# Branch projections by seven products, in one stream of weight steps with output projection and MLP

## The chip, the core and the metric

The kernel runs on one core of a Trainium2 chip. TensorE (PE in the profile) multiplies, with its weight loads on PEld; VectorE (DVE), ScalarE (ACT) and GpSimd (POOL) do the elementwise work; SyncE (SP) issues nearly all DMAs, ScalarE a few. The metric is device time of one execution in microseconds (us).

## What is computed

The reference is one decoder layer for 1024 tokens of width 1024, cut here to its frame. The three branches are a chunked mLSTM (M), a differential attention (D) and an attention to 256 memory tokens (C).

```python
h = rms_norm(x, norm_mix_g)
y_m, y_d, y_c = mlstm(h @ w_in[...]), diff_attention(h @ w_in[...]), cross_attention(h @ w_in[...], mem)
g_m, g_d, g_c = split(sigmoid(h @ w_gate + b_gate), 3)
merged = g_m * (y_m @ w_proj_m) + g_d * (y_d @ w_proj_d) + g_c * (y_c @ w_proj_c)
x = x + merged @ w_out
h2 = rms_norm(x, norm_mlp_g)
return x + square(relu(h2 @ w_up)) @ w_down
```

All weights of projections are 1024 x 1024; w_up is 1024 x 4096 and w_down 4096 x 1024. Everything is float32.

## The kernel before

Each float32 operand is split into two parts of lower precision: ACT casts the high part and DVE subtracts it for the low part (`split`, `split2`, lines 102 to 115). A product is then three matmuls (`mm3`, line 117): high times high, high times low, low times high. Activations lie transposed, features on the partitions and 512 tokens (one half, `hf`) in a matmul's columns.

The stages run one after the other on TensorE: norm and branch C, then branch M, 64 steps of gate groups, branch D, the rest of the gate groups, the three branch projections, the output projection, the MLP's up half and its down half. The gates come from a generator, `gate_steps`: each `next` gives one step of three matmuls `mm<-hT,w`. Steps are put between the branches' own work; a finished group passes ACT's tanh of half its value (`gt`, a sigmoid up to a factor) and is stored to DRAM (`gates<-gt`). Branch D projects a head group, turns queries and keys by PE (`pr`) into one buffer (`dsg`), sends that through SP's DMAs into `dq` and `dk`, and multiplies these to scores (`sc<-dk,dq`).

`tail` (line 1297) does the projections. It loads the branch's output (`kraw<-y`), splits it (`kt`) and goes through four column groups of 256 with eight k of 128 and four PSUM banks each (`group`, line 1274): 3 x 4 x 4 x 8 x 3 = 1152 matmuls `mm<-kt,w`. DVE multiplies a bank by 1 + gate (`gl`), POOL adds into `mg`; the sum is split into `mh` and `ml` and multiplied by `w_out` in 384 matmuls. Its use adds x, stores `x1_d` and, scaled, `h2_d`, and POOL sums the squares for the norm.

Up and down (`wino`, line 1174; `down`, line 1445) use a seven-product scheme. A pair of 128-blocks of k, a pair of column blocks and two halves of the tokens form 2 x 2 blocks; seven products of sums of blocks take the place of eight. The weights' sums are made by POOL (`wino_s`, four operations on 128x128, into `wraw`), the operands' by DVE and POOL (`wino_t`, `xts`); then all are split. A run is one output block: 4 pairs of k, 7 products of 3 matmuls each, 84 matmuls, into seven of PSUM's eight banks, so that a run's product can start when the run before has been read out of the bank. `PROD` is the order of products. The step table (`wino_steps`) loads and splits weights some steps ahead.

Where `pinned` is set, or an engine is wrapped in `InOrder`, instructions stand on their engine in the order in which the code writes them; elsewhere a scheduler sets the order. In both cases each engine and each DMA queue takes its instructions in that order. Tile pools hand out buffers; a pool that is opened in memory of a closed one makes its first writers wait for the last users of that memory.

After up, each output block passes the norm's scale (`rb`), relu and square (`rq`), and is stored with its sums (`r_d<-rq`, `r_d<-xts`); down loads it back (`xd<-r_d`), adds its four passes of each group in `acc` tiles, whose start is `x1_d` (`acc<-x_d`), and writes out.

Of the kernel before, what the change touches and what calls it, by code (L numbers as in the profile page):

```python
# [71 lines left out]
class Layer:  # L72
    def __init__(self, tc, a, out):
        self.tc, self.nc, self.a, self.out = tc, tc.nc, a, out
        self.V, self.A = InOrder(tc, tc.nc.vector), tc.nc.scalar
        self.n = 0
# [1044 lines left out]
    PROD = ((0, 0), (1, 2), (4, 4), (5, 5), (2, 6), (3, 3), (6, 1))  # L1121

    def wino_t(self, b, V):

        G = self.nc.gpsimd
        t = self.xtp.tile([P, 4, 512], F32, tag="xt", name=self.name("xts"))
        V.tensor_sub(t[:, 0], b[:, 0], b[:, 1])
        G.tensor_sub(t[:, 2], b[:, 2], b[:, 0])
        V.tensor_sub(t[:, 1], b[:, 2], t[:, 0])
        V.tensor_sub(t[:, 3], b[:, 3], t[:, 1])  # L1130
        return t

    def wino_x(self, kp, load):

        b = load(kp)
        t = self.wino_t(b, self.nc.vector)
        xo = self.xop[kp].tile([P, 7, 2, 512], F32R, tag="xo", name=self.name("xo"))
        self.split(xo[:, 0:3, 0], xo[:, 0:3, 1], b[:, 1:4])
        self.split(xo[:, 3:7, 0], xo[:, 3:7, 1], t)
        return xo  # L1140

    def wino_s(self, r):

        G = self.nc.gpsimd
        G.tensor_add(r[:, 4], r[:, 0], r[:, 3])  # L1145
        G.tensor_sub(r[:, 5], r[:, 4], r[:, 1])  # L1146
        G.tensor_sub(r[:, 6], r[:, 1], r[:, 0])  # L1147
        G.tensor_sub(r[:, 7], r[:, 2], r[:, 5])  # L1148

    def wino_steps(self, srcs, wrp, wop, lead):  # L1150


        raws, W = [], []

        def raw():
            n = len(raws)
            if n < len(srcs):
                r = wrp.tile([P, 8, P], F32, tag="wraw", name=self.name("wraw"))
                self.nc.sync.dma_start(r[:, 0:4], srcs[n])
                self.wino_s(r)  # L1160
                raws.append(r)

        def wsp(n, split=self.split2, more=True):
            m = len(W)
            if m < len(srcs) and m <= n + lead:
                wo = wop.tile([P, 7, 2, P], F32R, tag="wo", name=self.name("wo"))
                split(wo[:, :, 0], wo[:, :, 1], raws[m][:, 1:8])
                W.append(wo)
# [602 lines left out]
```

## Time and profile before

| what | us |
|---|---|
| runs: median of 3 | 2213.95 (2213.91 to 2215.54) |
| the profiled execution | 2213.57 |
| its span | 2211.8 |
| TensorE busy | 2163.4 (98%) |
| VectorE, ScalarE, GpSimd busy | 62%, 44%, 24% |
| 64 gate steps ahead of branch D, 192 matmuls | 575.5 to 620 |
| branch projections | 1218.5 to 1482.4 |
| output projection | 1482.4 to 1575.2 |
| up | 1575.2 to 1891.8 |
| down | 1891.8 to 2207.5 |

In rows of the profile, a group has its line of the code, its engine and operation, what it writes and reads, the count, then busy us and mean ns of one, and the idle time of the engine ahead of it with what ended it. A timeline row has its start, its length, and the same names. "SPq" rows are SP issuing DMAs.

### The profile page before, as it was taken

The page shows a single profiled execution, that of the slowest core. Times are in us where ns is not written, and L with a number is a line of the kernel's source. Part 1 is how long each engine was busy: PE and PEld are TensorE (multiplying, and loading weights), DVE is VectorE, ACT ScalarE, POOL GpSimd, SP SyncE. Part 2 cuts the span into 40 slices and gives each one's busy share as a digit, 9 for nine tenths or more (in the row PEclk, how much of TensorE's full clock was granted, in tenths as well). Part 3 has the DMA queues.
Part 4 walks back from the last instruction along what each step waited for, and adds up shares of the span by engine and source line. Part 5 has one row for each costly group of instructions (what it writes and reads, how often), then busy time and mean ns, then how long its engine had stood idle before and what let it go on. Part 6 is the DMA issues. An engine that isn't in the chain of part 4 may idle for free.

```text
span 2211.8 us, 30588 instructions
## 1 busy us (share of the span) xinstructions
PE 2163.4 (98%) x11097; PEld 1860.7 (84%) x11097; DVE 1361.4 (62%) x2598; ACT 980.7 (44%) x1962; POOL 527.8 (24%) x696
## 2 busy tenths in 40 slices
PE   7999999999999999999999999999999999899999
PEld 5878888898899999999888888877787888688887
DVE  6643575565237777777641232544688877767779
ACT  6543355454336666666542120223444444543332
POOL 2100000000011111111000003202557655565553
PEclk9999999999999999999999999999999999999999
DMA  7023122121333333333343443436435444854444
GB/s 250 29 81 115 50 91 76 44 82 39 107 109 86 93 84 84 88 92 86 101 148 114 134 142 126 138 110 205 147 115 198 159 147 147 318 196 146 145 145 170
DMA packets 127948, 273.06 MB, mean 123 GB/s; under 512 B 12945, under 2 KB 21430, under 8 KB 125750
## 3 DMA queue, kind: packets, MB, share of 16 engines
q1 hardware_dynamic: 125494, 258.53, 37.2%
q10 hardware_dynamic: 2304, 12.58, 1.4%
q8 instruction: 87, 1.43, 0.3%
q14 instruction: 63, 0.52, 0.1%
HBM read 178.76 MB, written 67.14 MB: 111 GB/s over the span
## 4 chain that ended last, share of the span: by engine, by line
PE 77%; DVE 9%; DMA 6%; ACT 4%; issue 2%; POOL 2%; SPq 0%; DVEq 0%; ACTq 0%; POOLq 0%
PE mm L91 46%; PE p L91 20%; PE sc L91 6%; PE tp L94 2%; PE po L91 2%; DVE acc L67 1%; DMA kraw<-y 1%; DMA xr<-h_d 1%; DVE wo L67 1%; DMA y<-yd 1%; DVE u L67 1%; DVE w L112 1%; DMA wraw<-in_wup 0%; DVE xts L67 0%; DVE c L67 0%
## 5 line engine op out<-in xcount | busy, mean ns | idle before, releaser
L91 PE MATMUL mm<-w,hT 128*128 128x384 f32 (+3 forms) x2496 | 473.4, 332 | 8.3 <-DVE dsg L112 5.4
L91 PE MATMUL mm<-hT,w 128*128 128x512 f32 x1920 | 465.7, 395 | 0.0
L91 PEld LDWEIGHTS mm<-hT,w 128*128 128x128 f32 x1920 | 353.5, 188 | 74.2
L91 PEld LDWEIGHTS mm<-w,hT 128*128 128x128 f32 x2496 | 389.2, 190 | 22.2 <-DVE dsg L112 7.6
L91 PE MATMUL p<-xd,wo 128*128 128x512 f32 x1344 | 310.0, 393 | 5.7 <-DVE c L67 2.2
L91 PE MATMUL p<-xo,wo 128*128 128x512 f32 x1344 | 308.2, 390 | 5.7 <-DVE st L1418 2.6
L91 PEld LDWEIGHTS p<-xd,wo 128*128 128x128 f32 x1344 | 253.8, 189 | 61.7 <-DVE c L67 3.3
L91 PEld LDWEIGHTS p<-xo,wo 128*128 128x128 f32 x1344 | 251.0, 188 | 61.5 <-DVE u L67 3.7
L91 PE MATMUL mm<-kt,w 128*128 128x512 f32 x1152 | 262.2, 389 | 1.9 <-ACT w L111 1.1
L112 DVE TENSOR_TENSOR w<-raw,w 128x256 fp32r<-128x256 f32 (+3 forms) x304 | 173.0, 590 | 137.9 <-ACT w L111 136.8
L91 PEld LDWEIGHTS mm<-kt,w 128*128 128x128 f32 x1152 | 216.0, 188 | 47.9 <-ACT w L111 1.5
L111 ACT CAST w<-raw 128x256 fp32r<-128x256 f32 (+3 forms) x304 | 154.3, 530 | 178.9 <-PE mm L91 114.5
L104 ACT CAST wo<-wraw 128x896 fp32r<-128x896 f32 x122 | 115.0, 945 | 208.9 <-PE p L91 115.2
L67 DVE TENSOR_TENSOR wo<-wraw,wo 128x896 fp32r<-128x896 f32 x122 | 143.7, 1195 | 59.4 <-ACT wo L104 59.4
L1145 POOL TENSOR_TENSOR wraw<-wraw 128x128 f32<-128x128 f32 x128 | 97.3, 760 | 245.8 <-DMA wraw<-in_wdown 108.1
L1007 ACT ACTIVATE dpe<-sc,dst,drr 128x256 f32<-128x256 f32 (+7 forms) x128 | 106.7, 834 | 99.7 <-DVE dst L1003 92.0
L999 DVE CUSTOM_DVE_ANT_0 sc<-sc,tmask 128x256 f32<-128x256 f32 (+7 forms) x128 | 97.0, 758 | 12.6 <-PE sc L91 12.5
L127 POOL TENSOR_SCALAR hss<-hss 128x4 f32<-128x4 f32 x8 | 3.3, 410 | 415.4 <-ACT mscr L752 272.9
L91 PE MATMUL sc<-dk,dq 128*128 128x512 f32 (+3 forms) x384 | 90.4, 343 | 0.0
L1148 POOL TENSOR_TENSOR wraw<-wraw 128x128 f32<-128x128 f32 x128 | 85.6, 669 | 10.0
L1146 POOL TENSOR_TENSOR wraw<-wraw 128x128 f32<-128x128 f32 x128 | 87.3, 682 | 0.0
L1147 POOL TENSOR_TENSOR wraw<-wraw 128x128 f32<-128x128 f32 x128 | 87.2, 682 | 0.0
(283 smaller groups left out, 2832.6 us busy)
## 6 DMA issues: line engine op xcount, KB each, us to landing
dk<-dsg SPq DMA_DIRECT2D x64, 256.0 KB, 4.4
wraw<-in_wup SPq DMA_DIRECT2D x64, 256.0 KB, 3.4
r_d<-xts SPq DMA_DIRECT2D x16, 1024.0 KB, 4.1
wraw<-in_wdown SPq DMA_DIRECT2D x64, 256.0 KB, 3.1
xd<-r_d SPq DMA_DIRECT2D x19, 768.0 KB, 7.4
xd<-r_d SPq DMA_DIRECT2D x14, 1024.0 KB, 6.8
raw<-in_wgate SPq DMA_DIRECT2D x48, 256.0 KB, 3.2
gates<-gt SPq DMA_DIRECT2D x48, 256.0 KB, 2.0
```

What stands on the lines that cost most here:

```text
L67: return self.tc.keep_in_program_order(f(*a, **k))
L91: self.pin(self.nc.tensor.matmul(out, l, r, start=start, stop=stop))
L94: self.pin(self.nc.tensor.transpose(out, x, self.ident))
L104: self.A.copy(hi, src)
L111: nc.scalar.copy(hi, src)
L112: nc.vector.tensor_sub(lo, src, f32(hi))
L999: V.tensor_tensor_reduce(out=sc[:, 0:n], in0=sc[:, 0:n], in1=self.tmask[:, D - n : D], scale=1.0, scalar=-3.0e38, op0=ALU.add, op1=ALU.max ...
L1007: nc.scalar.activation(pe[c][:, 0:n], sc[:, 0:n], AF.Exp, bias=t8[:, 2 + c : 3 + c], scale=rr[:, i, c : c + 1], accum_out=t8[:, 4 + c : 5 ...
L1145: G.tensor_add(r[:, 4], r[:, 0], r[:, 3])
L1146: G.tensor_sub(r[:, 5], r[:, 4], r[:, 1])
L1147: G.tensor_sub(r[:, 6], r[:, 1], r[:, 0])
L1148: G.tensor_sub(r[:, 7], r[:, 2], r[:, 5])
```

## The change

`tail`, `wino`, `wino_steps` and `down` are replaced by one function, `stream`. All weights from the branch projections on are one list of steps (48 of branches, 12 of the output projection, 64 each of up and down), loaded two steps at a time into two buffers and split three steps ahead into three. Every branch projection is four runs of 84 matmuls, in the order C, M, D. Operand tiles lie in slots that stages share (`SLOT`). The accumulators of down are placed in the left pool after `o`, the pool of `rq` and `xts`, has been closed.

The operands' sums of the branches are made ahead by `x_jobs` and kept in DRAM (`xtC_d`, `xtM_d`, `xtD_d`): C's and M's in eight jobs under the 64 gate steps, D's in eight half-jobs under the gate steps behind branch D. The counts in `waits` are gate steps between load, sums, store and the next load. `wino_t` works in place in a job. The first two operands and weights of the stream are prepared under the gates too (`s_early`).

```diff
+        self.G, self.S = InOrder(tc, tc.nc.gpsimd), InOrder(tc, tc.nc.sync)
...
-    PROD = ((0, 0), (1, 2), (4, 4), (5, 5), (2, 6), (3, 3), (6, 1))
+    PROD = ((1, 0), (2, 2), (5, 5), (0, 3), (3, 6), (4, 4), (6, 1))
+    SLOT = {"C": "ABCD", "M": "EABC", "D": "DEAB", "U": "ABHF", "N": "GABF"}
+    def wino_t(self, b, t, V, G):
+        V.tensor_sub(t[:, 1], b[:, 0], b[:, 1])
+        G.tensor_sub(t[:, 0], b[:, 2], b[:, 0])
+        V.tensor_sub(t[:, 2], b[:, 2], t[:, 1])
+        V.tensor_sub(t[:, 3], b[:, 3], t[:, 2])
+
+    def x_jobs(self, pool, jobs, n, waits):
+        nc = self.nc
+        for s, kp in jobs:
+            for c in range(0, 512, n):
+                r = pool.tile([P, 4, n], F32, tag="xj", name=self.name("xj"))
+                for k in range(2):
+                    src = self.yd[self.YOF[s]][2 * kp + k].rearrange("p (h n) -> p h n", h=2)
+                    self.S.dma_start(r[:, 2 * k : 2 * k + 2], src[:, :, c : c + n])
+                for _ in range(waits[0]):
+                    yield
+                self.wino_t(r, r, nc.vector, nc.gpsimd)
+                for _ in range(waits[1]):
+                    yield
+                self.S.dma_start(self.xtd[s][kp][:, :, c : c + n], r)
+                for _ in range(waits[2]):
+                    yield
...
+        def side(n):
+            self.w_split(n + 3)
+            for f in todo.pop(n, []):
+                f()
...
+        for n0, s in ((0, "M"), (16, "D")):
+            at(n0 + 5, self.x_load, s, 0)
+            at(n0 + 8, self.x_split, s, 0, (0,))
+            at(n0 + 9, self.x_split, s, 0, (1,))
+            for k in (1, 2, 3):
+                at(n0 + 11 + k, self.x_load, s, k)
+                at(n0 + 13 + k, self.x_split, s, k)
...
+        for u in range(16):
+            at(126 if u == 15 else 64 + 4 * u + (u == 0), up_rest, u)
+        at(110, self.x_load, "N", 0)
+        at(113, self.x_split, "N", 0, (0,))
+        at(114, self.x_split, "N", 0, (1,))
+        for q, l, m in ((1, 120, 122), (2, 121, 123), (3, 123, 125), (4, 124, 127)):
+            at(l, self.x_load, "N", q)
+            at(m, self.x_split, "N", q)
...
+        def accum():
+            left.close()
+            lp = L("acc")
+            accs.extend(lp.tile([P, 512], F32, name=f"acc{i}") for i in range(28))
+
+        at(126, accum)
...
-                        for _ in range(2 * 32):
+                    with tc.tile_pool(name="pg", bufs=2) as self.gpool, tc.tile_pool(name="xj", bufs=2) as xj:
+                        jobs = self.x_jobs(xj, [("C", k) for k in range(4)] + [("M", k) for k in (3, 2, 1, 0)], 512, (5, 3, 0))
+                        for _ in range(2 * 32):
+                            next(jobs, None)
                             next(self.gates)
+                        for _ in jobs:
+                            pass
...
+                    with tc.tile_pool(name="pgh", bufs=2) as self.gpool, tc.tile_pool(name="xjd", bufs=1) as xj:
+                        jobs = self.x_jobs(xj, [("D", k) for k in range(4)], 256, (5, 2, 4))
+                        early = self.s_early()
                         for _ in self.gates:
+                            next(early, None)
+                            next(jobs, None)
...
-            self.tail()
+            self.stream()
```

`up_rest(15)` makes and stores the last `xts`; `use_up` writes `rq`. What the change does to the order of instructions is shown at three places, all on SP.

The first is the start of branch D. Before, SP's queue holds these rows there: gate stores, D's weights (`in_wd`), and D's own loads.

```order
L472 DMA gates<-gt_5970 128x512
L472 DMA gates<-gt_5998 128x512
L903 DMA raw_6282<-in_wd 128x768
L903 DMA raw_6284<-in_wd 128x768
L903 DMA raw_6346<-in_wd 128x768
L472 DMA gates<-gt_6026 128x512
L903 DMA raw_6820<-in_wd 128x768
L882 DMA dq_6224<-dsg_6248 64x512 x4
L894 DMA dk_6225<-dsg_6306 64x2x512 x4
```

In the changed kernel the same place holds the last four jobs (`xj`, of M), each with its load and its store (`xtM_d`).

```order
L67 DMA xtM_d<-xj_5950 128x2048
L67 DMA xj_5986<-y 128x1024 x2
L905 DMA raw_6412<-in_wd 128x768
L905 DMA raw_6886<-in_wd 128x768
L67 DMA xtM_d<-xj_5986 128x2048
L67 DMA xj_6022<-y 128x1024 x2
L67 DMA xtM_d<-xj_6022 128x2048
L67 DMA xj_6058<-y 128x1024 x2
L67 DMA xtM_d<-xj_6058 128x2048
L884 DMA dq_6290<-dsg_6314 64x512 x4
L896 DMA dk_6291<-dsg_6372 64x2x512 x4
```

D's loads of queries and keys stand behind three loads and four stores of M's sums.

The second place is the end of the gate groups, where the branch projections begin. Before, the projections' operands are loaded there as `kraw` and gates as `gl`.

```order
L472 DMA gates<-gt_12716 128x512
L472 DMA gates<-gt_12744 128x512
L472 DMA gates<-gt_12772 128x512
L1305 DMA gl_13063<-gates 128x512
L472 DMA gates<-gt_12800 128x512
L1305 DMA gl_13067<-gates 128x512
L1268 DMA kraw_12948<-y 128x1024
```

In the changed kernel the last two half-jobs of D (`xj_12879`, `xj_12924`) stand there, among the loads of C's third and fourth operand (`xo_13050`, `xo_13054`).

```order
L67 DMA xj_12879<-y 128x2x256 x2
L67 DMA xo_13050<-y 128x512
L67 DMA xtD_d<-xj_12879 512x1x256
L474 DMA gates<-gt_12994 128x512
L67 DMA xo_13050<-y 128x1024
L67 DMA xj_12924<-y 128x2x256 x2
L67 DMA xo_13050<-xtC_d 128x2048
L67 DMA xtD_d<-xj_12924 512x1x256
L67 DMA xo_13054<-y 128x512
L67 DMA xo_13054<-y 128x1024
L67 DMA xo_13054<-xtC_d 128x2048
```

Parts of both operands' loads have moved behind the two stores.

The third place is the start of down. Before, six accumulators are loaded ahead of the last store of `xts`.

```order
L1556 DMA acc_17979<-x_d 128x512
L1556 DMA acc_17984<-x_d 128x512
L1159 DMA wraw_18239<-in_wdown 128x512
L1408 DMA r_d<-xts_17930 128x2048
L1556 DMA acc_17982<-x_d 128x512
L1159 DMA wraw_18276<-in_wdown 128x512
```

In the changed kernel that store comes first.

```order
L67 DMA wraw_18092<-in_wdown 128x512 x2
L67 DMA r_d<-xts_18099 128x2048
L67 DMA acc_18113<-x_d 128x512
L67 DMA acc_18118<-x_d 128x512
L67 DMA acc_18116<-x_d 128x512
L67 DMA acc_18117<-x_d 128x512
L67 DMA wraw_18211<-in_wdown 128x512 x2
```

All accumulator loads have moved behind the store of the last `xts`, and that behind the load of one more pair of weights.

807 lines of the change are left out of this document (385 added, 422 removed).

## The prediction

> **What bounds the kernel now.** I read the page first, then TensorE's timeline, then the waits around the three places that the change rebuilds. In the page's rows see that TensorE (PE) is busy for 98% of the span, and that the three groups which the change touches hold it for 262, 310 and 308 us. Whatever stalls PE, or takes matmuls away, therefore shows in the time one for one.
>
> ```profile
> span 2211.8 us, 30588 instructions
> PE 2163.4 (98%) x11097; PEld 1860.7 (84%) x11097; DVE 1361.4 (62%) x2598; ACT 980.7 (44%) x1962; POOL 527.8 (24%) x696
> ...
> L91 PE MATMUL p<-xd,wo 128*128 128x512 f32 x1344 | 310.0, 393 | 5.7 <-DVE c L67 2.2
> L91 PE MATMUL p<-xo,wo 128*128 128x512 f32 x1344 | 308.2, 390 | 5.7 <-DVE st L1418 2.6
> ...
> L91 PE MATMUL mm<-kt,w 128*128 128x512 f32 x1152 | 262.2, 389 | 1.9 <-ACT w L111 1.1
> ```
>
> The sum is made against this execution: 2211.8 of span and 1.77 around it, 2213.57 in all, which is 0.4 below the median of the runs, 2213.95.
>
> PE's timeline gives the pitch. In the second row see 469 matmuls in one stretch without a wait: (106.47 − 0.39) / 468 = **0.2267 us** from one to the next. The first row is the last gate groups, which lead up to them without a wait.
>
> ```profile
> 1151.72 66.94 PE L91 MATMUL mm<-hT,w 128*128 128x512 f32 x294
> 1218.50 106.47 PE L91 MATMUL mm<-kt,w 128*128 128x512 f32 x469
> ```
>
> **What goes.** A branch projection by seven products takes 4 groups × 4 pairs of k × 7 × 3 = 336 matmuls for 384. Three branches: 144 fewer × 0.2267 = **−32.6**.
>
> The output projection keeps its 384 matmuls but takes its weights from the stream. The rows show what two late weight splits cost before.
>
> ```profile
> 1529.52 0.50 PE L91 MATMUL mm<-mh,w 128*128 128x512 f32 x1 [0.73 <-ACT w L111]
> ...
> 1533.26 1.22 PE L91 MATMUL mm<-mh,w 128*128 128x512 f32 x2 [3.00 <-DVE w L112]
> ...
> 1536.86 0.62 PE L91 MATMUL mm<-mh,w 128*128 128x512 f32 x2
> ```
>
> The idle is 0.73 + 3.00, and the ten matmuls behind the longer one take 1536.86 − 1533.26 = 3.60 us, where the pitch gives 2.27: 1.3 more. That is 5.0; with weights three steps ahead I leave 0.5, so **−4.5**. Between no gain and all of it: 0 to −5.
>
> The MLP's up half runs from the first row below to the second, 316.6 us for 1344 × 0.2267 = 304.7, an excess of 11.9, of which 5.7 is idle (the page's row) and the rest px matmuls of the norm (about 3.9) and pace. Its operands are now loaded earlier and its weights summed in fewer POOL operations; the norm's wait stays (I leave 3.6 at its head). **−4.4**, bounds 0 and −6.
>
> ```profile
> 1575.17 6.28 PE L91 MATMUL p<-xo,wo 128*128 128x512 f32 x27
> ...
> 1891.75 0.84 PE L91 MATMUL p<-xd,wo 128*128 128x512 f32 x3
> ...
> 1902.72 304.75 PE L91 MATMUL p<-xd,wo 128*128 128x512 f32 x1329 [0.70 <-DVE c L67]
> ```
>
> **What comes, 1: branch D starts late.** C's and M's operand sums (x_jobs) are put under the 64 gate steps ahead of branch D. Eight matmul-triples, 24 × 0.2267 = 5.44 us, stand for one job. A job is: load 2 × 512 KB, DVE, POOL, DVE, DVE in series (each writes over what the last one read), store 1 MB. The next load stands behind that store on SP, which takes its instructions in order.
>
> ```profile
> kraw<-y SPq DMA_DIRECT2D x24, 512.0 KB, 4.5
> ...
> r_d<-xts SPq DMA_DIRECT2D x16, 1024.0 KB, 4.1
> raw<-in_wgate SPq DMA_DIRECT2D x48, 256.0 KB, 3.2
> ...
> acc<-x_d SPq DMA_DIRECT2D x16, 256.0 KB, 6.0
> ```
>
> A cycle by these rows: 4.5 to land, 0.7 for two issues, three DVE operations of 128x512 at 0.69, POOL 1.3 to 1.8 (rows in part 4), 0.4 to issue: about **9.3 against 5.44**. Started at 576, C's four end near 614 and M3 near 623; the gates end at 620. M2's second half stands on DVE behind branch D's third reduction, M1's first behind the four draw multiplies: their rows of before are these.
>
> ```profile
> 638.13 2.91 POOL L128 TENSOR_TENSOR drr<-drr,mhalf 128x16 f32<-128x16 f32 x1
> ...
> 640.39 2.47 SPq L882 DMA_DIRECT2D dq<-dsg  x4
> ...
> 641.08 0.90 DVE L887 TENSOR_TENSOR draw<-draw,drr 128x128 f32<-128x128 f32 x4
> ...
> 646.46 3.45 SPq L894 DMA_DIRECT2D dk<-dsg  x4
> ...
> 652.81 0.33 PE L91 MATMUL sc<-dk,dq 128*128 128x128 f32 x2
> ```
>
> So M1 goes on at 642.0 and is stored at 646.0; M0 is loaded at 646.3, has landed at 651, is stored near 654.9 and lands 4.1 later, at 659. Branch D's dq load stands behind that store on SP (the order shows it) and takes memory that the jobs held, so it issues at 659, not 640.4. Before, the first score came 652.81 − 640.39 = 12.4 later: 671.4. PE has nothing else in its order: **+18.6**. Least, with loads landing in 3.2: about 14; most, with 6.0: about 24.
>
> **2: the stream starts late.** D's sums are eight half-jobs under the last gates, one buffer: load 3.2 + 0.4, work 2.6, store 0.3, and the store must land (2 to 4, I take 2.8) before the next load: 9.3 us. Eleven triples, 7.5 us, stand for one. Eight lag 14.4 by the end, and 98 triples hold 10 more than 88 (6.8): the last load is near 1229. C's operands for the third and fourth pair of k stand behind those jobs on SP and DVE. The third is due at 1218.5 + 2 × 4.76 = 1228.0, and ready near 1238.3: 10.3, then 0.9 and 0.7 for the next two splits. **+12**; bounds 0, if each store lands at once, and 18.
>
> **3: between branches**, DVE splits three operands in three consecutive steps (14 to 16 and 30 to 32).
>
> ```profile
> L67 DVE TENSOR_TENSOR wo<-wraw,wo 128x896 fp32r<-128x896 f32 x122 | 143.7, 1195 | 59.4 <-ACT wo L104 59.4
> ...
> L67 DVE TENSOR_TENSOR u<-u,p 128x512 f32<-128x512 f32 x75 | 50.2, 686 | 5.8
> ...
> L67 DVE TENSOR_TENSOR xd<-xd 128x2048 fp32r<-128x2048 f32 x12 | 29.2, 2436 | 0.0
> ...
> L67 DVE TENSOR_TENSOR xd<-xd 128x1536 fp32r<-128x1536 f32 x16 | 28.8, 1799 | 0.0
> ```
>
> 3 × (1.80 + 2.44 + 1.20) + 7 × 0.69 + 4 × 0.69 = 23.9 of DVE in 3 × 4.76 = 14.3 of PE. Of the 9.6 over, one step's lead covers 4.8; twice the rest: **+9** (0 if the lead is two steps, 19 if none).
>
> **4: DVE and POOL want the same operands' memory.** The rows show pairs of operations that meet.
>
> ```profile
> L1347 POOL TENSOR_TENSOR mg<-mg,gl x16: 1282/1285/1299, 1327.2 to 1394.2; 128x512 f32<-128x512 f32 x16
> ```
>
> ```profile
> 1747.69 0.69 DVE L67 TENSOR_TENSOR xts<-rq 128x512 f32<-128x512 f32 x1 [1.62 <-ACT rq L1404]
> ...
> 1750.88 2.62 DVE L67 TENSOR_TENSOR wo<-wraw,wo 128x896 fp32r<-128x896 f32 x2
> ```
>
> ```profile
> 1747.73 1.81 POOL L1128 TENSOR_TENSOR xts<-rq 128x512 f32<-128x512 f32 x1
> ...
> 1751.24 1.31 POOL L1146 TENSOR_TENSOR wraw<-wraw 128x128 f32<-128x128 f32 x1
> ...
> 1756.84 0.46 POOL L1145 TENSOR_TENSOR wraw<-wraw 128x128 f32<-128x128 f32 x1 [3.02 <-DMA wraw<-in_wup]
> ```
>
> A POOL sum of 0.46 takes 1.31 beside DVE's splits, and 1.29 becomes 1.81 beside DVE's 0.69. If such pairs run strictly one after the other, one branch run of 19.04 us (84 × 0.2267) in M or D needs: splits 4 × 1.09, gates 4 × 0.69, a quarter of a branch's operand splits 4.2, and on POOL eight weight sums of 0.73 (between 0.46 and 1.29 by size) and four merges of 1.29, in all 22.3 for M and, with 2.8 of other splits in place of 4.2, 20.9 for D: 4 × 3.3 + 3 × 1.9 = 19 over. Weights stand two pairs ahead, about 16 us of lead, so I take **+3**; bounds 0 and 19. The Trainium skill ("SBUF — State Buffer", section "SBUF: two separate sides") states that DVE, in operations with two SBUF inputs, and GpSimd take a shared port pair as an exclusive lock for a whole instruction; these rows agree, and by that rule the time is that of the third rival below.
>
> **5: down starts late.** Before, 15 matmuls took 1902.72 − 1891.75 = 10.97, a loss of 7.6; the loads of the first accumulators were issued ahead of the last xts store.
>
> ```profile
> 1912.90 4.80 SPq L1556 DMA_DIRECT2D acc<-x_d  x6
> ...
> 1918.84 1.29 POOL L1128 TENSOR_TENSOR xts<-rq 128x512 f32<-128x512 f32 x1
> ...
> 1920.15 0.32 SPq L1408 DMA_DIRECT2D r_d<-xts  x1
> ...
> 1921.46 0.69 DVE L67 TENSOR_TENSOR acc<-acc,acc 128x512 f32<-128x512 f32 x1 [2.91 <-DMA acc<-x_d]
> ```
>
> Now they stand behind it, and lie in memory that xts holds. From the end of up's step 122: three operand splits make steps 124 and 127 late by 2.2 and 1.1. The last xts stands on POOL behind sums of weights whose load waits for a split near 32; xts is done at 40.5, stored, landed at 44.7 (4.1), and the accumulators land at about 49. DVE's subtraction and first add free the bank of step 128's third product at 50.4, due at 35.7: 14.7. The later three groups of loads stand behind weight loads: about 1.3 each. 22 in place of 7.6: **+14**; bounds +5 (loads at once) and +18.
>
> **6: pace behind long waits.** Above, ten matmuls lost 1.3 behind a 3.00 wait; two long waits stand ahead of dense matmuls: **+2.6**. The Trainium skill ("TensorE: Matmul & The Clock Gate", "What's actually happening") says that one idle window of about 3.4 us halves the clock for about 3.4 us; by that it would be, as an estimate, 1.7 each, 3.4. The trace shows the kind, not the size.
>
> Sum: −32.6 − 4.5 − 4.4 = −41.5; 18.6 + 12 + 9 + 3 + 14 + 2.6 = +59.2. Net +17.7 on 2213.6: about **2231**.
>
> **Rivals.** *Faster: the jobs hide.* The place is SP's queue at branch D and at the stream's start; the point is a job cycle under 5.44 us (7.5 for half-jobs). Then 18.6, 12 and 1.3 go: 2199. For it: DVE is 62% busy and POOL hardly used there. Against: landing alone takes 4.5 of 5.44. *Down starts as before*: if the accumulators' loads come early, 14 goes: 2217. For it: waits listed in an order may long be met; against: the store stands ahead of them in one queue. *DVE and POOL exclude each other and the lead is spent*: +16 more, 2247. For: the rows above; against: the same pairs in up left PE with 5.7 idle. *The change does its matmuls but both of the first two hold*: 2185.
>
> **How the numbers follow.** Forecast 0.52 (own range 2219 to 2241), jobs hidden 0.12, down as before 0.14, exclusion 0.14, both first 0.04, other 0.04 above. About 0.2% (4.4 us) is what a measurement of this kernel tells from no change. Faster holds 0.12 + 0.04 and 0.04 of down as before with shorter stalls: 0.20; same 0.10 of that case and 0.05 of the forecast's lower end: 0.15; slower 0.65. The range, 2206 to 2248, leaves out the hidden jobs and the far end of exclusion.
>
> **What would show it.** Right: the first sc<-dk,dq some 18 us later behind the same gates, dq<-dsg issued behind an xtM store; a PE wait near 10 in the third step of the first run; waits behind acc<-x_d at the second run of down; 1008 products of branches at the old pitch. Wrong: job cycles near 5.4, PE without waits at those places, or a longer pitch in M and D.

## The result, and the profile after

The changed kernel takes **2336.99 us** (median of four runs, 2335.49 to 2337.79) beside 2214.74 for the kernel before (2213.91 to 2215.70) on the same chip: 1.0551 times as long, with an interval of 1.0533 to 1.0569. It is slower, as forecast, but by 122 us, not by 17, and far outside the range.

The page of the changed kernel answers to the first rows of before:

```profile
span 2334.7 us, 30365 instructions
...
PE 2171.2 (93%) x10953; PEld 1852.5 (79%) x10953; DVE 1493.0 (64%) x2732; ACT 1022.1 (44%) x1991; POOL 591.6 (25%) x564
...
L93 PE MATMUL p<-xo,wo 128*128 128x512 f32 x3696 | 884.1, 401 | 97.1 <-DVE acc L67 24.7
...
L93 PE MATMUL mm<-w,hT 128*128 128x384 f32 (+3 forms) x2496 | 477.4, 334 | 33.9 <-DVE dsg L114 26.3
```

There are 144 matmuls fewer (10953 for 11097), yet TensorE is busy 7.8 us longer: 2171.2, where 2163.4 − 32.6 = 2130.8 was to be expected, so 40.4 us went into matmuls at a lower pace. Its idle time, span less busy, went from 48.4 to 163.5, 115.1 more. 115.1 + 40.4 − 32.6 = 122.9, the difference of the spans (2334.7 − 2211.8). Nearly all idle time of the stream stands in one group, `p<-xo,wo`, which holds branches, up and down: 97.1 us.

By stages, from the starts in PE's timeline:

| stage | before, us | after, us | difference | forecast |
|---|---|---|---|---|
| up to the branch projections | 1218.5 | 1252.6 | +34.1 | +18.6 |
| branch projections | 263.9 | 285.7 | +21.8 | −32.6 + 12 + 9 + 3 = −8.6 |
| output projection | 92.8 | 86.8 | −6.0 | −4.5 |
| up | 316.6 | 335.5 | +18.9 | −4.4 |
| down | 315.7 | 369.8 | +54.1 | +14 |

After the change, the output projection is taken to end with its last matmul at 1625.1, so up's first wait counts as up's. The forecast's 2.6 of pace behind long waits belongs to no one stage. PE's timeline of the changed kernel at five places: branch D's start, the stream's start, the changes of branch, up's start and down's start. In brackets stands the wait ahead of each row and what ended it.

```profile
619.40 8.51 PE L93 MATMUL mm<-w,hT 128*128 128x384 f32 x48
632.37 13.85 PE L93 MATMUL mm<-w,hT 128*128 128x384 f32 x63 [4.46 <-DVE dv L114]
...
674.26 8.73 PE L93 MATMUL mm<-w,hT 128*128 128x384 f32 x36 [21.14 <-DVE dsg L114]
682.83 0.33 PE L93 MATMUL sc<-dk,dq 128*128 128x128 f32 x2
...
1275.17 0.79 PE L93 MATMUL p<-xo,wo 128*128 128x512 f32 x1 [12.18 <-ACT xo L67]
1280.05 2.93 PE L93 MATMUL p<-xo,wo 128*128 128x512 f32 x6 [4.09 <-DVE xo L67]
...
1359.00 1.65 PE L93 MATMUL p<-xo,wo 128*128 128x512 f32 x3 [4.30 <-ACT u L67]
...
1448.16 1.65 PE L93 MATMUL p<-xo,wo 128*128 128x512 f32 x3 [4.30 <-ACT u L67]
...
1476.37 11.81 PE L93 MATMUL p<-xo,wo 128*128 128x512 f32 x38 [4.85 <-DVE c L67]
...
1629.53 1.22 PE L93 MATMUL p<-xo,wo 128*128 128x512 f32 x2 [4.07 <-ACT wo L67]
...
1974.25 1.65 PE L93 MATMUL p<-xo,wo 128*128 128x512 f32 x3 [12.96 <-ACT u L67]
...
2019.14 21.60 PE L93 MATMUL p<-xo,wo 128*128 128x512 f32 x84 [9.09 <-DVE acc L67]
2045.38 22.10 PE L93 MATMUL p<-xo,wo 128*128 128x512 f32 x84 [4.64 <-DVE acc L67]
2073.18 21.89 PE L93 MATMUL p<-xo,wo 128*128 128x512 f32 x84 [5.69 <-DVE acc L67]
2100.37 230.03 PE L93 MATMUL p<-xo,wo 128*128 128x512 f32 x1002 [5.30 <-DVE acc L67]
```

The waits are where the prediction put them: ahead of the first score (682.83, before 652.81, so +30.0), at the third step of the first run (12.18), between the branches (4.30, 4.30, 4.85) and at the second run of down (9.09). Of the 34.1 us ahead of the branch projections 30.0 stand ahead of the first score; most of the rest are waits for ACT's `gt` in the last gates (2.44 and 0.66), which a run without D's jobs (e2) doesn't have. Two places are new: up's start, and an early wait of 12.96 in down, both on operands.

SP's queue in the changed kernel, around branch D's start (start, length of the issue, what is loaded or stored):

```profile
586.39 0.32 SPq L67 DMA_DIRECT2D xtC_d<-xj  x1
...
597.28 0.33 SPq L67 DMA_DIRECT2D xtC_d<-xj  x1
...
654.32 0.32 SPq L67 DMA_DIRECT2D xtM_d<-xj  x1
...
664.63 0.32 SPq L67 DMA_DIRECT2D xtM_d<-xj  x1
668.53 2.48 SPq L884 DMA_DIRECT2D dq<-dsg  x4
```

The eight stores of the jobs lie 78.24 us apart in all, 11.2 from one to the next, not 9.3. `dq` is issued 3.9 behind the last of them, as the prediction said, but at 668.53 instead of 659. The page's landings and the windows of the DMA engines say why. In a landing row stand count, size of one and median us; in a window row the window, its length, the busy times of the five engines, the granted clock, the DMA engines' busy share and GB/s.

```profile
xo<-r_d SPq DMA_DIRECT2D x19, 1024.0 KB, 9.2
...
xj<-y SPq DMA_DIRECT2D x16, 512.0 KB, 6.3
```

```profile
575.00:620.00 45.00, 45.00 (x205) 37.48 (x204) 14.18 (x27) 12.92 (x26) 6.41 (x6) 1.00 0.85 283
...
1356.00:1360.00 4.00, 1.00 (x2) 0.83 (x3) 2.85 (x2) 3.44 (x4) 0.00 (x0) 0.80 1.01 410
...
1970.00:1974.00 4.00, 0.00 (x0) 0.00 (x0) 2.02 (x2) 2.98 (x3) 0.00 (x0) 0.50 1.01 426
```

The kernel before, in the first of these windows:

```profile
575.00:620.00 45.00, 45.00 (x202) 36.85 (x200) 9.73 (x20) 14.33 (x29) 1.25 (x2) 1.00 0.41 131
```

A load of 512 KB took 4.5 us before and takes 6.3 here; one of 1 MB takes 9.2. The DMA engines are 85% busy under the jobs, where they were 41% busy before, and full at the change of branch and at down's start.

### The profile page after: what moved, and what is told of

It reads as the page before. It is cut to its first block, busy times and chain, and to the rows that moved or that the text cites. A ratio compares the mean times of both kernels' runs of the same rounds, so it can differ in the third digit from the quotient of the medians.

```text
span 2334.7 us, 30365 instructions
## 1 busy us (share of the span) xinstructions
PE 2171.2 (93%) x10953; PEld 1852.5 (79%) x10953; DVE 1493.0 (64%) x2732; ACT 1022.1 (44%) x1991; POOL 591.6 (25%) x564
## 4 chain that ended last, share of the span: by engine, by line
PE 66%; DMA 11%; DVE 10%; ACT 4%; issue 4%; POOL 3%; SPq 2%; DVEq 0%; POOLq 0%; ACTq 0%
PE mm L93 29%; PE p L93 25%; PE sc L93 5%; DMA xj<-y 4%; PE po L93 3%; DVE wo L67 2%; PE tp L96 2%; SPq L67 1%; POOL wraw L67 1%; DVE u L67 1%; DVE gl L67 1%; DMA acc<-x_d 1%; ACT xo L67 1%; DMA y<-yd 1%; DMA gl<-gates 1%
## 5 line engine op out<-in xcount | busy, mean ns | idle before, releaser
L93 PE MATMUL p<-xo,wo 128*128 128x512 f32 x3696 | 884.1, 401 | 97.1 <-DVE acc L67 24.7
L93 PEld LDWEIGHTS p<-xo,wo 128*128 128x128 f32 x3696 | 709.9, 193 | 270.0 <-DVE acc L67 26.4
L67 POOL TENSOR_TENSOR wraw<-wraw 128x256 f32<-128x256 f32 x352 | 370.9, 1064 | 538.8 <-DMA wraw<-in_wdown 198.2
L93 PEld LDWEIGHTS mm<-w,hT 128*128 128x128 f32 x2496 | 392.8, 191 | 48.3 <-issue 21.4
L67 ACT CAST wo<-wraw 128x896 fp32r<-128x896 f32 (+1 forms) x186 | 172.4, 932 | 455.3 <-PE p L93 277.1
L67 DVE TENSOR_TENSOR wo<-wraw,wo 128x896 fp32r<-128x896 f32 (+1 forms) x186 | 231.4, 1250 | 149.3 <-ACT wo L67 148.8
L67 DVE TENSOR_TENSOR xo<-xo 128x1536 fp32r<-128x1536 f32 (+1 forms) x58 | 124.3, 2153 | 32.7 <-ACT xo L67 32.5
L67 ACT CAST xo<-xo 128x1536 fp32r<-128x1536 f32 (+1 forms) x58 | 97.3, 1691 | 47.3 <-DMA xo<-y 26.1
L67 DVE TENSOR_TENSOR u<-u,p 128x512 f32<-128x512 f32 x140 | 93.7, 686 | 12.0 <-PE p L93 0.5
L93 PE MATMUL po<-mh,wo 128*128 128x512 f32 x256 | 78.9, 389 | 0.0
L93 PE MATMUL po<-dv,daT 128*128 128x256 f32 x576 | 75.4, 274 | 0.6 <-DVE daT L114 0.6
```

Source lines behind the costliest of these rows:

```text
L67: return self.tc.keep_in_program_order(f(*a, **k))
L93: self.pin(self.nc.tensor.matmul(out, l, r, start=start, stop=stop))
```

## Experiments

The theory at the outset was that the time comes from loads and stores that are issued too late, in the order of one queue, at the four places that the prediction names. The rival was that it comes from work and bytes: that the stages hold more than fits into them, whatever the order. Each kernel ran once, beside one run of the kernel before (2214.8 with e1 to e4, 2214.6 with e5 to e8, 2211.5 with e9 to e12, 2216.2 with e13 and e14, 2213.3 with the rest). These runs of one kernel lie 4.7 us apart, so differences of 2 or 3 us mean nothing. Where something is left out, the result is no longer the layer's, and the time says only what the part costs. Differences are against 2337.0.

### The jobs: e1, e2, e3

e1 and e2 leave the jobs out and load the branches' outputs where the sums would be loaded, in the same number of bytes. This is e1's edit:

```diff
-        dma(f32(t[:, 1, 3:7]), self.xtd[s][kp])
+        if s in "CM":
+            src = self.yd[self.YOF[s]][2 * kp : 2 * kp + 2].rearrange("k p (h n) -> p k h n", h=2)
+            for k in range(2):
+                dma(f32(t[:, 1, 3 + 2 * k : 5 + 2 * k]), src[:, k])
...
-                        jobs = self.x_jobs(xj, [("C", k) for k in range(4)] + [("M", k) for k in (3, 2, 1, 0)], 512, (5, 3, 0))
+                        jobs = self.x_jobs(xj, [], 512, (5, 3, 0))
```

> Left out: the operand sums of C and M (no jobs under the 64 gate steps; the stream reads as many bytes of the branch outputs in their place). Theory (SP takes the eight jobs one after the other at 11.2 us a job, and branch D's dq load stands behind the last store): the first sc<-dk,dq is back at 653 from 682.8 and the 4.5 us wait for dv goes; the projections begin near 1222 in place of 1252.6, and the whole takes about 2305. Rival (the late start comes of DVE's and POOL's order, or of the 1.3% more bytes, not of the jobs): D starts late all the same, 2330 or more.

Measured 2309.66, 27.3 less. PE's timeline of e1:

```profile
654.45 0.33 PE L93 MATMUL sc<-dk,dq 128*128 128x128 f32 x2
...
1247.90 0.80 PE L93 MATMUL p<-xo,wo 128*128 128x512 f32 x1 [12.90 <-ACT xo L67]
```

The first score is back to within 1.6 us of before (652.81). The wait at the stream's start stays, so it isn't of these jobs. e2 is the same edit for D.

> Left out: the operand sums of D (no half-jobs under the last gates; the stream reads as many bytes of the branch output in their place). Theory (C's third and fourth operand wait behind the half-jobs' stores and loads): the waits of 12.2, 4.1, 1.4 and 1.8 in the first run of the stream go, with the slow clock behind them some 25 us, so about 2310; branch D still starts at 683. Rival (C's operands are late because 1 MB lands in 8 us, whatever stands ahead): the first run still waits over 10 us, 2325 or more.

Measured 2314.47, 22.5 less; of the waits at the stream's start 1.03 and 1.72 are left. Both places are the jobs'. e3 asks whether only their order is at fault: it computes everything and loads two jobs ahead into three buffers. C's and M's sums and stores also come sooner behind their loads, 3 and 2 gate steps in place of 5 and 3.

```diff
+        for i in range(ahead):
+            load(i)
+        for i, (s, kp, c) in enumerate(todo):
...
+            self.S.dma_start(self.xtd[s][kp][:, :, c : c + n], tiles[i])
+            load(i + ahead)
```

> Whole computation. The jobs load two ahead, with three buffers for two (C, M) and three for one (D). Theory (the cycle of a job is the sum of landing, sums and store because the next load stands behind the store): a job now takes what its sums take, 4 to 5 us, and branch D and the stream start nearly on time; 30 + 25 us go, about 2285. Rival (landing at 6.3 us a load is bandwidth, so jobs stay as slow): under 15 us go, 2322 or more.

Measured 2305.92, halfway between theory and rival: 31 less, where leaving out both sorts of jobs is worth 27.3 + 22.5. The stream's start is nearly mended (1.77 us left), branch D's is not: its first score comes at 672.5. PE's longest wait in e3 under the gates, and the window there:

```profile
607.85 1.22 PE L93 MATMUL mm<-hT,w 128*128 128x512 f32 x2 [9.86 <-ACT w L113]
```

```profile
576.00:624.00 48.00, 35.78 (x143) 27.85 (x142) 18.01 (x31) 7.34 (x16) 10.17 (x9) 0.86 0.95 363
```

The DMA engines are 95% busy at 363 GB/s, and PE now waits there (35.78 busy of 48) for the gates' own weights. Eight jobs move 8 × 2.1 = 16.8 MB; under 192 matmuls, 43.5 us, that is 386 GB/s. The kernel before moved 131 there, so the two come to 517, over the 426 of the fullest window shown here. At this place the rival holds: these bytes do not fit under the gates, whatever their order.

### Down: e4, e6, e15, e16

e4 loads down's operands ahead of the store of `xts` in their step, puts the first accumulators into memory that is free earlier, and issues their loads on ACT's queue. e6 also splits the second and third operand a step later. e15 is the changed kernel with the accumulators of the second to fourth group loaded one run ahead, and e16 is e6 with that.

```diff
-        for u in range(16):
-            at(126 if u == 15 else 64 + 4 * u + (u == 0), up_rest, u)
         at(110, self.x_load, "N", 0)
...
+        for u in range(16):
+            at(126 if u == 15 else 64 + 4 * u + (u == 0), up_rest, u)
...
+            t = [lp.tile([P, 512], F32, name=f"acc{i}") for i in range(28)]
+            accs.extend(t[13:27] + t[0:13] + t[27:])
...
-                    S.dma_start(acc[j], half(self.x1d, 2 * g + f, hf))
+                    A.dma_start(acc[j], half(self.x1d, 2 * g + f, hf))
```

> Whole computation. Down's operand loads stand ahead of the xts store in their step, the accumulators of the first two groups lie in memory that xsH held, not xts, and all accumulator loads go by ACT's queue. Theory (waits of 13.0, 4.3, 3.3, 9.1, 4.6, 5.7 and 5.3 are order and memory): some 45 us of down go, about 2292. Rival (the loads of 1.75 MB land in 7 to 9 us each and bound it): only what waits for accumulators goes, about 25, 2312.

> Whole computation. As e4_down_order, and the splits of down's second and third operand one step later, behind the sums of the last run of up. Theory (same mechanism: ACT's copy waits behind the cast of an operand that has not landed): the waits of 5.3 and 6.8 us in e4_down_order shrink to under 4 in sum, about 2300. Rival (the loads land too late for PE anyway): the wait only moves to the operand's first product, 2306 or more.

e4 measured 2307.79 (29.2 less), nearer its rival's 2312 than its theory's 2292. e6 measured 2300.84 (36.2 less), as its theory had it, but not by the waits that it named. PE's timeline of e6:

```profile
1964.84 1.66 PE L93 MATMUL p<-xo,wo 128*128 128x512 f32 x6 [1.49 <-DVE xo L67]
...
1985.74 0.80 PE L93 MATMUL p<-xo,wo 128*128 128x512 f32 x1 [6.49 <-ACT xo L67]
...
2018.51 20.93 PE L93 MATMUL p<-xo,wo 128*128 128x512 f32 x84 [3.93 <-DVE acc L67]
```

The 12.96 was 5.30 in e4 and is 1.49 here. In the changed kernel, ACT's `u` stands there behind the cast of an operand whose load SP issues at 1962.77, right behind a store of `xts`; e4 brings the load forward, and e6 takes the cast out of the copy's way. The 9.09 is gone with e4, which changes the order, the memory and the queue of the accumulators at once, so these three aren't told apart. A wait for an operand is left, 6.81 in e4 and 6.49 here.

```diff
-                for j, f, hf in ((1, 0, 1), (6, 0, 0), (4, 1, 1), (5, 1, 0)):
-                    S.dma_start(acc[j], half(self.x1d, 2 * g + f, hf))
+                for h in range(g + (g > 0), min(g + 2, 4)):
+                    for j, f, hf in ((1, 0, 1), (6, 0, 0), (4, 1, 1), (5, 1, 0)):
+                        S.dma_start(accs[7 * h + j], half(self.x1d, 2 * h + f, hf))
```

> The changed kernel with one edit: the accumulators of down's second to fourth column group are loaded one run (about 20 us) ahead of their use; nothing is left out. Theory (those three waits, 4.64, 5.69 and 5.30, come from loads that are issued in the run that uses them; the slow pace behind each costs 1.5 to 2.7 more): the three waits go, about 2316. Rival (DVE's own chain in down holds the bank): the waits stay, now behind another DVE name, 2333 or more.

Measured 2315.10, 21.9 less, as expected to a microsecond. PE's timeline of e15 runs on from the second run of down without a further wait (the view ends at 2230):

```profile
2022.06 208.19 PE L93 MATMUL p<-xo,wo 128*128 128x512 f32 x908 [9.77 <-DVE acc L67]
```

That settles three of down's waits: each load of accumulators was issued in the run that uses it. Of the 21.4 us by which the span shrinks, 7.5 are busy time (2163.7 for 2171.2): pace that came back with them.

> e6 with the same edit; nothing is left out. Theory: the waits of 3.93, 2.32 and 2.66 go with their slow pace (84 matmuls in 20.9 for 19.2), about 2287 against e6's 2300.8. Rival: no change, 2300.

Measured 2301.45: a miss. PE's timeline of e16:

```profile
2008.19 222.13 PE L93 MATMUL p<-xo,wo 128*128 128x512 f32 x970 [9.09 <-ACT acc L67]
```

The three later waits did go, and one of 9.09 on ACT took their place. In e6 these loads are on ACT's queue; eight of them now stand ahead of ACT's copies that free the banks. ACT's timeline of e16:

```profile
1998.25 9.26 ACTq L67 DMA_DIRECT2D acc<-x_d  x3
2007.55 1.56 ACT L67 COPY acc<-p 128x512 f32<-128x512 f32 x3 [14.68 <-DMA r_d<-xts]
```

The last three loads are held until a store of `xts` has landed, and the copies behind them with it. The edit on SP wasn't run with e6.

### The changes of branch: e5, e9, e10, e12, e13

PE waits there behind a copy by ACT (`u`). e5 takes it that the copy stands behind a late split, and splits the three operands a step later. ACT's timeline of the changed kernel shows the copy behind two casts, for which ACT waits until the operand has landed:

```profile
1354.08 1.47 ACT L67 CAST xo<-xo 128x1536 fp32r<-128x1536 f32 x1 [3.84 <-DMA xo<-y]
1356.57 1.90 ACT L67 CAST xo<-xo 128x2048 fp32r<-128x2048 f32 x1 [1.01 <-DMA xo<-xtM_d]
1358.37 0.58 ACT L67 COPY u<-p 128x512 f32<-128x512 f32 x1
```

```diff
-                at(n0 + 13 + k, self.x_split, s, k)
+                at(n0 + 14 + k, self.x_split, s, k)
```

> Whole computation. The splits of the second to fourth operand of M and D come one step later (steps 15 to 17 and 31 to 33 for 14 to 16 and 30 to 32). Theory (an operand of 1.75 MB takes 8 to 10 us to land; ACT, in order, waits for it and holds up its copy of the finished bank, for which PE waits 4.3 us twice): both waits go, with the slow pace behind them 8 to 12 us, about 2327. Rival (the prediction's: DVE has 23.9 us of work in 14.3 us of PE there, whatever stands where): no gain or worse, 2337 to 2345.

Measured 2339.26: that fell, and the rival held. The waits moved from ACT's copy to the splits themselves (2.26, 3.90, 2.25 and 6.02, all on DVE's `xo`), so a later place alone gives nothing. Three kernels take work away, each of one kind: DVE's low parts of M's and D's second to fourth operand (e9), POOL's merges of the branches (e10), the loads of these operands' sums (e12).

```diff
+            if s in "MD" and kp:
+                self.A.copy(t[:, 0, c], f32(t[:, 1, c]))
+                continue
```

```diff
-                if s == "M":
-                    G.tensor_add(mg[k], mg[k], t)
-                elif s == "D":
-                    (V if u == 3 else G).tensor_add(t, mg[k], t)
+                if s == "D" and u == 3:
+                    V.tensor_add(t, mg[k], t)
```

```diff
-        dma(f32(t[:, 1, 3:7]), self.xtd[s][kp])
+        if s in "CU" or kp == 0:
+            dma(f32(t[:, 1, 3:7]), self.xtd[s][kp])
...
```

e12 then splits the loaded blocks in three pieces in place of two.

> Left out: the low parts (DVE's subtraction) of the second to fourth operand of M and D, six operands, 25 us of DVE. Theory (DVE bounds PE between the branches, as the prediction had it: 23.9 us of work in 14.3): the waits of 4.3 us at both changes of branch and those behind them go, 12 to 18 us less, about 2322. Rival (ACT waits there for operands that land late, and its copy of the bank with it): those waits stay, 2332 or more.

> Left out: POOL's additions of M's and D's gated products to the sum (28 of 1.29 us). Theory (POOL and DVE exclude each other on operands in SBUF, so POOL's merges and weight sums run late and hold the ring's tiles that DVE writes next): the wait of 4.85 us at D's second run and the 1.3 to 1.6 us waits around it go, 6 to 12 us less, about 2328. Rival (POOL's work lies beside everything): under 2 us, 2335.

> Left out: the loads of the operands' sums (1 MB of 1.75 MB each) for the second to fourth operand of M and D; the splits are as many, of the blocks that are loaded. Theory (between the branches three operands of 1.75 MB, weights and gates come at 406 to 417 GB/s with all DMA engines busy, and ACT's copy waits behind the cast of the operand that lands last): the two waits of 4.3 us on ACT's u go or shrink to 1, with the pace behind them 8 to 12 us less, about 2327. Rival (DVE's and POOL's work sets it): the waits stay over 3, 2333 or more.

Measured 2327.21, 2325.09 and 2334.91. Within the traces the output projection starts 7.4, 14.8 and 0.1 us earlier than the changed kernel's 1538.3. PE's timeline of e9:

```profile
1356.53 61.21 PE L93 MATMUL p<-xo,wo 128*128 128x512 f32 x255 [3.76 <-ACT u L67]
...
1444.27 21.62 PE L93 MATMUL p<-xo,wo 128*128 128x512 f32 x87 [4.90 <-ACT u L67]
```

Without DVE's low parts the two waits of 4.30 are still 3.76 and 4.90: that half of e9's theory fell, and only shorter waits behind them went. In e10 the 4.85 is gone, as its theory had it, and the 4.30s are 3.34 and 3.98. Without the bytes the waits only moved (2.71, 1.26, 2.70, 1.51, 3.96), so the full DMA engines at 1356 alone do not bound this place. e13 does e5, e9 and e10 at once.

> Left out: POOL's additions of M's and D's products, and the low parts of the second to fourth operand of M and D; their casts come one step later. Theory (between the branches several waits of like size stand in one chain, load, cast, copy, subtraction, merge, so that one taken away gives way to the next): together they give more than apart, 12 us of e10 and 10 of e9 and something of e5, about 2307, and no wait over 2 us at the changes of branch. Rival (they are independent): 22 us, and the waits of 4.3 on ACT's copy stay, 2315 or more.

Measured 2305.14, 31.9 less; the output projection starts at 1508.0, 30.3 earlier, which is more than 7.4 + 14.8. PE's timeline of e13 behind the first change of branch:

```profile
1359.58 148.59 PE L93 MATMUL p<-xo,wo 128*128 128x512 f32 x654 [0.31 <-DVE u L67]
```

654 matmuls without a wait, at (148.59 − 0.39) / 653 = 0.2270 us, the pitch of before. What bound the changes of branch is a chain of three: ACT's casts of operands that land late, DVE's low parts behind the casts, and POOL's merges. Each taken away alone leaves others. e9 and e10 together without e5 weren't run. How DVE and POOL meet is in POOL's timeline of the changed kernel (not of e13), and in its windows of the same two stretches, whose columns are as above:

```profile
1464.73 7.19 POOL L67 TENSOR_TENSOR wraw<-wraw 128x256 f32<-128x256 f32 x4 [10.03 <-DMA wraw<-in_wpd]
1471.89 3.71 POOL L67 TENSOR_TENSOR mg<-mg,gl 128x512 f32<-128x512 f32 x3
1475.55 3.04 POOL L67 TENSOR_TENSOR wraw<-wraw 128x256 f32<-128x256 f32 x4
```

```profile
1464.73:1471.92 7.19, 6.79 (x30) 5.28 (x29) 4.66 (x7) 1.54 (x2) 7.03 (x5) 1.00 0.39 105
1475.55:1478.59 3.04, 2.22 (x5) 1.84 (x6) 2.06 (x3) 0.00 (x0) 2.88 (x6) 0.50 0.64 222
```

Four sums of weights take 7.19 us while DVE splits and gates for 4.66 us, and 3.04 while it reads PSUM for 2.06. The merges behind the 7.19 release DVE's `c`, which waits 5.80 us for them, and that releases PE's bank: the wait of 4.85 in the first timeline. Ahead of the 7.19 POOL had sat idle for 10.03 us with the merges behind it in its order. It waited for weights whose load SP issued only at 1461.06, when DVE's split of 1459.91 had freed their buffer.

### Up's start: e7

```diff
-        self.wino_t(b, b, self.V, self.G)
+        self.wino_t(b, b, self.V, self.V)
```

> Whole computation. The one sum of up's operands that POOL made goes to DVE. Theory (up starts late because that sum stands on POOL behind weight sums and squares, 15 us of work): the waits of 4.1 and 1.3 at up's start go, about 2330. Rival (up starts late for the norm's chain or its weights): under 2 us, 2335.

Measured 2328.04, 9.0 less; the waits of 4.07 and 1.26 at up's head are gone. This is half of up's 18.9; the other half wasn't tried. Up's operand sum stood on POOL behind four sums of squares (7.02 us) and four sums of weights (3.07).

### Other places for the jobs, and all at once: e8, e11, e14, e17, e18

e8 and e11 compute everything and have e3's loads ahead, e6's down and e7's edit. e8 also has e5's later split, and puts C's jobs into branch M. e11 keeps C's under the gates and puts M's into branch D. From e11's edit:

```diff
+    def after(self, n, g):
+        for _ in range(n):
+            yield
+        yield from g
...
+                            self.side_jobs = self.after(70, self.x_jobs(jm, [("M", k) for k in (3, 2, 1, 0)], 128, (8, 6, 6), 1))
```

> Whole computation. All of the above, and C's jobs are moved into branch M in pieces of 128 columns, M's alone stay under the 64 gate steps, loads go ahead of stores. Theory (16.8 MB of the eight jobs in 43.5 us would be 386 GB/s, over the 338 to 342 that this kernel ever moved; half of it fits): branch D starts within 5 us of before, and with the other parts about 100 us go: 2235. Rival (the jobs cost by their order on DVE and SP, not by their bytes): branch D is late by 10 or more, 2250 or more.

> Whole computation. C's jobs alone stay under the 64 gate steps, M's go into branch D in pieces of 128 columns, D's with loads ahead; down's order of e6 and up's sum on DVE as in e7. Theory (half the bytes fit under the 64 steps): the first sc<-dk,dq at 652 to 657, the stream's start at 1225 or before, and of the 123 us lost some 85 are back: about 2253. Rival (any job in front of branch D delays it): first score after 665, 2265 or more.

Measured 2282.34 and 2270.51. e8 missed by 47 us (and its 338 to 342 GB/s were no bound, as the 410 and 426 above show): the jobs weren't done by the end of branch M, which grew by 9 us, and PE then waited for the gates' weights (15.57); branch D's first score came at 679.7. In e11 it comes at 656.0, as its theory had it, so half of the bytes do fit under the gates. The time missed its 2253 by 17 us all the same: branch D itself, from first score to last, takes 476.3 us for 465.6. e17 adds the accumulators' loads ahead, as in e16.

> e11 with the same edit; nothing is left out. Theory: its waits of 5.27, 2.38 and 2.00 go with their slow pace, 2256 to 2259 against 2270.5, still slower than the kernel before. Rival: no change, 2270.

Measured 2254.06: the fastest that computes everything, 40.8 above the kernel before. e14 takes every named cause away: all jobs, the low parts, the merges, with e5, e6 and e7. e18 adds the accumulators' loads.

> Left out: all operand sums ahead of the stream (as in e1 and e2), and what e13 leaves out; down in e6's order and up's sum on DVE. Theory (the loss of 123 us is made of the jobs, the changes of branch, up's start and down's start, each with slow pace behind its waits): the parts add up, 50 + 30 + 9 + 36 = 125 us less, about 2212, and TensorE's busy time falls from 2171 toward the 2131 that 144 matmuls fewer would leave. Rival (a part of the loss lies in the stream itself, in its pace or its weight steps): 2235 or more.

> e14 with the same edit (left out: the sums of the branches' operands, the low parts of those of M and D but their first, and the merges). Theory: the waits of 3.41, 3.14 and 2.96 go with their slow pace, about 2208, so that with every named stall away the seven products give a little, but less than the 32.6 of their matmuls. Rival: a pace that is slower everywhere holds the rest, 2217 or more.

e14 measured 2222.09 and e18 2215.28, beside 2216.18 and 2213.29 for the kernel before. e14 is 114.9 below the changed kernel, so the parts that it takes away hold nearly all of the 122; it came out nearer its theory's 2212 than its rival's 2235. e18's gain over the kernel before didn't come: its 2215.28 is nearer the rival's 2217 than 2208. The page and PE's timeline of e18:

```profile
PE 2143.6 (97%) x10953; PEld 1840.2 (83%) x10953; DVE 1432.1 (65%) x2676; ACT 1021.1 (46%) x1991; POOL 521.2 (24%) x516
```

```profile
1902.97 0.79 PE L93 MATMUL p<-xo,wo 128*128 128x512 f32 x1 [6.83 <-ACT xo L67]
...
1920.86 287.88 PE L93 MATMUL p<-xo,wo 128*128 128x512 f32 x1257 [8.98 <-ACT acc L67]
```

The output projection of e18 starts at 1458.3, 24.1 earlier than before, and up starts 30.0 earlier. All of that is lost again in up and down, 8.98 of it to the edit's own wait on ACT and 6.83 to the operand that e6 left; the rest is in shorter waits and pace. So seven products are only level with eight in this stream, although e18 leaves out the new work and, with the merges and low parts, some that the kernel before does too.

## Why the prediction was right in its sign and wrong in its size

The direction and the places were right. What failed is the size of every term that adds time, and the sign of up's. The largest misses are down (+14 for 54.1), pace behind waits (+2.6 for 40.4, part of which lies in the other terms), the changes of branch (12 for 31.9), up (−4.4 for +18.9) and branch D's start (+18.6 for 30.0). Of the removed work, the matmuls and the output projection came out. The runs' prices below include the pace lost behind each wait.

- **What goes.** −32.6 for 144 matmuls holds: 10953 are left, and in e13 they run at 0.2270. The output projection's −4.5 came to −6.0. **Up's −4.4 was wrong in sign**, +18.9: I counted the POOL operations that were saved and not the queue in front of the one that PE needs. Up's operand sum moved behind the norm's squares on POOL; e7 shows 9.0 of it, and the rest stays open.
- **"Branch D starts late", +18.6.** Right mechanism (jobs longer than their place, and D's `dq` behind the last store), mis-sized: +30.0 at the first score, 27.3 in e1. The term took the job's load at 4.5, from a row of stages that moved less, and it took 6.3; the last store came at 664.63 and not at 654.9. Both bounds, 14 and 24, were bounds of the same kind. The sum of the stage's bytes, 16.8 MB in 43.5 us, was in reach and wasn't made; by e3 and e11 it decides what an order can win back.
- **"The stream starts late", +12.** Mis-sized: 22.5 in e2. The waits there are 12.18, 4.09, 1.38 and 1.76 for 10.3, 0.9 and 0.7. D's half-job stores come 10.2 us apart (1206.18 to 1277.39), not 9.3. The second wait is for the third operand's second part: SP issues its load at 1272.16, behind the last half-job's load, and ACT waits 4.96 for it, until 1280.08. The term had no separate landing for that part.
- **"Between branches", +9, and "DVE and POOL want the same operands' memory", +3.** Together 12 for 31.9 in e13. I set them down as two terms and let the weights' lead absorb the second. Term 3 also had the wait wrong: it counts DVE's work alone, and e9 leaves both waits of 4.30, which are ACT's copy behind casts of operands that land late. At the second run of D the trace shows one chain: the weights come late behind DVE's splits, DVE's splits stretch POOL's sums from 3.04 to 7.19, the merges behind them hold DVE's `c`, and `c` holds PE's bank. Both terms' full prices, 9 and 19, come to 28, so the third rival was nearest in size. The Trainium skill ("SBUF — State Buffer", section "SBUF: two separate sides") has DVE and GpSimd lock a shared port pair for a whole instruction when DVE reads two SBUF inputs. By that, 3.04 of POOL and 4.66 of DVE would take 7.70 one after the other; 7.19 was measured, so the trace agrees nearly in full. No run tells this lock from the mere amount of work, since e9 and e10 take away work and overlap at once.
- **"Down starts late", +14.** The wait ahead of the second run is the one that I named, and e4 and e6 remove it; it came to 9.09 for the 14.7 of the working. But the term held, beside it, 3.3 for splits and an estimate of 1.3 for each later group; measured were 12.96, 4.28 and 3.31 ahead of it, the first two for operands, and 4.64, 5.69 and 5.30 for the later groups (21.9 in e15). Missed altogether: down's own operand load stands behind a store of `xts` too, the one at 1962.39, and such loads of 1 MB took 9.2 us to land.
- **"Pace behind long waits", +2.6.** The mis-sized step that touches all others: 40.4. Its unit was low too: I counted ten matmuls behind the wait of 3.00, and the rows show nine, so 3.60 us stand for 9 × 0.2267 = 2.04, a loss of 1.6 and not 1.3. In the windows of the changed kernel, for `p` on PE alone, see the granted clock behind the wait of 9.09 (PE busy and count, clock, DMA share, GB/s):

```profile
2019.00:2023.00 4.00, 3.86 (x9) 0.50 0.00 0
2023.00:2027.00 4.00, 4.00 (x17) 0.87 0.01 4
2027.00:2031.00 4.00, 4.00 (x19) 1.00 0.60 189
```

The run behind it takes 21.60 us where 83 × 0.2267 + 0.39 = 19.2: 2.4 more. The Trainium skill ("TensorE: Matmul & The Clock Gate", section "What's actually happening") gives half the clock for about 3.4 us, by which, as an estimate, 1.7 us are lost; the trace agrees in kind and shows some more. What the forecast missed is the count: two long waits were priced, and waits of 4.64 to 5.69 cost as much (22.10 and 21.89 for the same 84). Even behind e6's waits of 3.93 and 2.32 the run takes 20.93 and 20.95, 1.7 more. Across the runs the busy time falls as the waits go: 2171.2, 2163.3 in e6, 2156.0 in e17, 2143.6 in e18.

The rivals of a faster kernel are out: the jobs came 11.2 us apart, not 5.44, and in e3, where six of the stores come 5.9 apart, TensorE waits for the gates' weights instead. Down's start didn't stay as before either. The range rested on durations of a kernel whose DMA engines were half idle.

## What to carry to other kernels

When a change puts loads and stores under a stage, sum the stage's bytes over its time first: medians of landings come from stretches with room, and stretch as soon as the stage is full. In these runs a wait of 4.6 us or more on TensorE cost its length and 2.4 to 2.9 us of pace behind it, and one of 2.3 to 3.9 still 1.7, so waits have to be counted and not only added up. Before an operation is moved to a queue, list what stands ahead of it there: up's sum on POOL, down's operand on SP, and in an experiment the accumulators' loads on ACT each made a wait that the saved work did not show.

## What the runs showed of the hardware that was not expected

- The 16 DMA engines moved 410 and 426 GB/s at a busy share of 1.01 in 4 us windows; loads of 1 MB (`xo<-r_d`) took 9.2 us to land in the median; under the jobs 363 GB/s at 0.95 in e3.
- The clock stood at 0.50 for about 4 us behind a wait of 9.09 us, and waits of 4.64 to 5.69 us cost the run behind them as much: 2.7 to 2.9 us in 84 matmuls. In e6 even a wait of 2.32 was followed by a clock of 0.50 (2043 to 2045) and cost 1.7.
- Four POOL sums of 128x256 took 3.04 us beside DVE operations that read PSUM, and 7.19 beside ones that read two operands from SBUF. Of the 7.19 the first sum took 4.55 and ended at 1469.28, just after DVE had paused at 1468.67; DVE's weight splits beside it took 1.08 each, as at other places.
